# Twenty-seven of the first feed-forward matrix's 32 blocks as seven half-size products for eight

## The chip, the core and the metric

The kernel runs on one core of a Trainium2 chip. TensorE multiplies (weights stationary, tokens moving, sums in PSUM); ScalarE, VectorE and GpSimd do the elementwise work; SyncE (SP) issues most transfers from memory. Each engine works through its own queue. The metric is the time of one execution on the device in microseconds. Three runs of the kernel before took 1827.59, 1828.64 and 1833.59 us; their median is 1828.64 us.

## The reference

One layer of a recurrent decoder trunk for a prompt of 256 tokens and 8 samples of 4 tokens, 288 tokens in all, with a model width of 2048. Everything is float32. The part at issue is the last one, the feed-forward with its norm and its conditioned shift, scale and gate:

```python
mod = jax.nn.silu(c) @ P['w_ada'] + P['b_ada']
sh1, sc1, gt1, sh2, sc2, gt2 = [m[:, None, :] for m in jnp.split(mod, 6, axis=-1)]
...
x = x + gt1 * mix
xn = rmsnorm(x, P['g_norm2']) * (1.0 + sc2) + sh2
x = x + gt2 * (jnp.square(jax.nn.relu(xn @ P['w_ff1'])) @ P['w_ff2'])
...
y = rmsnorm(x, g_final)
```

`w_ff1` is 2048 x 8192 and `w_ff2` 8192 x 2048. Both are read once, for all 288 tokens.

## The kernel before

Features lie on the 128 partitions and the 288 tokens along the free axis (`N` = 288). A float32 product is made of three float16 products: a weight tile of 128 x 1024 is converted to a high part by ScalarE (`to_parts`, L210) and a low part by VectorE (`rest`, L134, one scalar-tensor-tensor operation that also writes a column of sums for a later check), the tokens are split the same way, and TensorE adds high x high, high x low and low x high in PSUM (L301).

The feed-forward (`feed_forward`, from L2001) goes over 256 *visits*. A visit is one weight tile of 128 x 1024, 512 KB, and 24 matmuls of 128 x 128 weights with 288 columns of tokens. The hidden width is cut into eight parts `hb`. For each there are four blocks of the first matrix (`ff1`, 256 outputs each, two PSUM banks, four visits) and four of the second (`ff2`, 512 outputs, four banks, four visits). `order` lists them: the first matrix for part `hb`, then the second for part `hb - 1`. A first-matrix block ends in `ev` of `ff1`: relu and square on ScalarE, a square and the low part on VectorE, into the tiles `hx`. A second-matrix block is added into the accumulator `facc` by VectorE (L1940), for the first part by ScalarE copies (L1936).

At step `v` the program first lets `convert` run until the tiles of five visits are ahead, then multiplies visit `v`, then evacuates a block that is complete. `convert` of one tile issues the transfer of a later tile into the buffer that it frees (`fetch`, on SP's queue). `in_order` chains the instructions of TensorE, ScalarE and VectorE in the order in which the program issues them; GpSimd's are ordered by the planner. PSUM has eight banks: four of the pool `mm`, two `px`, one `pi`, one `pa`.

Beside the visits run the last units of the adaLN product, those of the gate `gt2`: each loads 1 MB of `w_ada`, and `step` acts on letters that are repeated over the visits: L loads a unit, C converts a part of it, v multiplies it. In `cond_parts` a unit is converted to float16 parts (ScalarE L449, VectorE L134) and multiplied in 16 float16 matmuls (L466); in `cond_product` it is multiplied as float32, without conversion (L418). `half_resid` multiplies the accumulator by the gate and adds the residual on GpSimd (L1924 to L1927), at the end of the second matrix's blocks of part 6. `certificates` checks the columns of sums from all low parts against bounds with some VectorE operations and small matmuls (L144 to L150); if a bound is missed, the whole trunk is run a second time in a slower form.

Ahead of the feed-forward, `scaled` (L1857) and `sumsq` (L638) work on GpSimd for the second norm, and `second_norm` (L1895 to L1899) produces the tokens' two parts `zh` and `zl` in the first four steps.

Of the kernel before, what the change touches and what calls it, by code (L numbers as in the profile page):

```python
# [8 lines left out]
F32 = mybir.dt.float32  # L9
# [45 lines left out]
def trunk(ctx, tc, io, fast):  # L55
# [96 lines left out]
    def certificates():  # L152

        yield from certify(0, mixed[0], 8.0)
        yield from certify(704, mixed[1], 2.0 ** -3)
        done_ = list(mixed)
        for at_ in (150, total - 24, total - 5):
            while now[0] < at_:
                yield
            upto = list(marks)  # L160
            yield from certify(done_[0], upto[0], 8.0)
            if upto[1] > done_[1]:
                yield from certify(done_[1], upto[1], 2.0 ** -3)
            done_ = upto
# [101 lines left out]
    def in_order():  # L266
# [4 lines left out]
        for i in traced[n:]:  # L271
# [3 lines left out]
            if i.engine in (mybir.EngineType.PE, mybir.EngineType.Activation, mybir.EngineType.DVE):  # L275
                queued[i.engine] = i
# [8 lines left out]
    class Block:  # L285

        def __init__(self, w, blk, g0, width, act, evac):
            self.w, self.blk, self.g0, self.act, self.evac = w, blk, g0, act, evac
            self.nm_t, self.kg = width // P, 1024 // width
            self.ps = None  # L290

        def multiply(self, g, hi, lo, ms, kks):
            if self.ps is None:
                self.ps = [bank() for _ in range(self.nm_t)]
            hi, lo = (t_.rearrange("p (k m) -> p k m", k=self.kg) for t_ in (hi, lo))
            for m in ms:
                for kk in kks:
                    k = self.kg * g + kk
                    xh, xl = self.act(k)
                    for i, (a, x) in enumerate(((hi, xh), (hi, xl), (lo, xh))):  # L300
                        pace["last"] = T.matmul(self.ps[m][:, :N], a[:, kk, m * P:(m + 1) * P], x, start=k == 0 and i == 0,  # L301
                                                stop=k == 4 * self.kg - 1 and i == 2)

# [210 lines left out]
    def ada_half(name, kind, h):  # L514
# [6 lines left out]
        if fast and name != "sj0":  # L521
# [1388 lines left out]
    def ff1(hb):  # L1910
        for b in range(4):
# [8 lines left out]
            yield Block(io["wf1"], 4 * hb + b, 0, 256, lambda k: (zh[:, k, :], zl[:, k, :]), ev)  # L1920
# [8 lines left out]
    def ff2(hb):  # L1929
        x = hx[hb % 2]  # L1930
        for b in range(4):
            def ev(m, p, b=b):
# [6 lines left out]
                if hb < 7:  # L1939
                    V.tensor_tensor(out=a, in0=a, in1=p, op=ALU.add)  # L1940
                    if hb == 6:
# [6 lines left out]
            yield Block(io["wf2"], b, 4 * hb, 512, lambda k: (x[0][:, k, :], x[1][:, k, :]), ev)  # L1948

    blocks = []  # L1950
    for hb in range(9):
        if hb < 8:
            blocks.extend(ff1(hb))
        if hb:
            blocks.extend(ff2(hb - 1))
# [218 lines left out]
```

## Time and profile before

| | |
|---|---|
| median of three runs | 1828.64 us (1827.59 to 1833.59) |
| profiled execution, its time | 1828.35 us |
| profiled execution, span from first to last instruction | 1826.6 us |
| mean granted TensorE clock | 0.991 |
| instructions | 38533 |

The span is that of one execution; the 1.75 us that its time has beyond it lie around the first and the last instruction. In the rows that follow, PE is TensorE, PEld its weight loads, ACT is ScalarE, DVE is VectorE and POOL is GpSimd. A row of a group has the line of the program, engine and operation, output and inputs with shapes and types, the count, then busy time in us and mean ns of one, then the idle time ahead of it with what ended it. A row of the timeline begins with the start and the duration in us. A row of a stretch has its bounds, its length, and the busy time of PE, PEld, DVE, ACT and POOL with their counts, then the clock, the DMA share and GB/s.

### The profile page before, as it was taken

To read this page: it belongs to the slowest core of one execution; us is meant where nothing else is said; L and a number is where in the kernel's file an instruction comes from. 1 tells how busy PE (TensorE), PEld (TensorE's weight loads), DVE (VectorE), ACT (ScalarE), POOL (GpSimd) and SP (SyncE) were. 2 spreads that over 40 slices of the span, in tenths; PEclk is the share of its full clock that TensorE was granted. 3 is DMA by queue.
4 is the path that set the end of the run, shared out by engine and by line. 5 is a ranking of instruction groups with operands and counts; after the bars stand their busy time and mean duration, and the time that the engine had idled before them with its cause. 6 is when DMAs were issued, how large, how long until landed. Compare 5 with 4: busy or idle time off the path is not lost.

```text
span 1826.6 us, 38533 instructions
## 1 busy us (share of the span) xinstructions
PE 1775.3 (97%) x15792; PEld 1377.2 (75%) x15792; DVE 1183.4 (65%) x2568; ACT 901.8 (49%) x1252; POOL 211.2 (12%) x281
## 2 busy tenths in 40 slices
PE   8999999999999999999999899999999999999996
PEld 6787667786777877677777677777777777777785
DVE  4777855645685568687677876556665566555565
ACT  5334384545455455366555565554544454443443
POOL 0002201110133010001113500000000000000171
PEclk9999999999999999999999899999999999999998
DMA  9999767547855459977778556566656556555541
GB/s 392 414 410 337 262 226 258 208 155 268 282 177 184 163 197 323 312 242 261 252 286 316 184 195 198 197 204 215 204 198 217 203 197 203 173 183 176 184 151 55
DMA packets 113290, 422.97 MB, mean 232 GB/s; under 512 B 11648, under 2 KB 11936, under 8 KB 109904
## 3 DMA queue, kind: packets, MB, share of 16 engines
q1 hardware_dynamic: 97744, 364.18, 56.7%
q0 software_dynamic: 10608, 39.64, 6.2%
q10 hardware_dynamic: 4752, 16.60, 2.3%
q8 instruction: 125, 2.05, 0.4%
q14 instruction: 61, 0.50, 0.1%
HBM read 403.56 MB, written 16.81 MB: 230 GB/s over the span
## 4 chain that ended last, share of the span: by engine, by line
PE 65%; DVE 2%; DMA 1%; issue 1%; ACT 1%; POOL 0%; DVEq 0%; ACTq 0%; POOLq 0%
PE mm L301 33%; PE mm L237 20%; PE pi L301 8%; PE pa L466 1%; DMA st<-mC 1%; DVE pair L134 0%; PE px L1629 0%; DMA s<-mC 0%; PE px L1715 0%; DMA o_C_s<-st 0%; PE pi L1698 0%; PE px L1639 0%; DVE s L2051 0%; PE px L1570 0%; PE px L1558 0%
## 5 line engine op out<-in xcount | busy, mean ns | idle before, releaser
L237 PEld LDWEIGHTS <-pair 128*128 128x128 f16 x6528 | 631.8, 98 | 202.3 <-issue 22.0
L301 PEld LDWEIGHTS <-pair 128*128 128x128 f16 x6144 | 601.3, 98 | 159.4 <-issue 7.1
L237 PE MATMUL mm<-x,pair 128*128 128x288 f16 x4320 | 563.3, 287 | 7.1 <-DVE pair L134 2.8
L134 DVE SCALAR_TENSOR_TENSOR pair<-raw,pair 128x1024 f16<-128x1024 f32 x250 | 308.3, 1235 | 224.4 <-ACT pair L224 130.5
L301 PE MATMUL mm<-hx,pair 128*128 128x288 f16 x2472 | 321.0, 286 | 0.0
L301 PE MATMUL mm<-z,pair 128*128 128x288 f16 x2448 | 313.4, 288 | 3.3 <-ACT z L1899 2.9
L134 DVE SCALAR_TENSOR_TENSOR pair<-xl,pair 128x1024 f16<-128x1024 f32 x165 | 202.9, 1231 | 150.1 <-ACT pair L224 91.1
L224 ACT ACTIVATE pair<-raw 128x1024 f16<-128x1024 f32 x163 | 171.6, 1054 | 217.4 <-PE mm L237 136.5
L134 DVE SCALAR_TENSOR_TENSOR pair<-s,pair 128x1024 f16<-128x1024 f32 x113 | 140.2, 1242 | 123.2 <-ACT pair L210 123.1
L224 ACT ACTIVATE pair<-xl 128x1024 f16<-128x1024 f32 x109 | 114.9, 1054 | 164.2 <-PE mm L237 96.4
L210 ACT ACTIVATE pair<-s 128x1024 f16<-128x1024 f32 x113 | 119.0, 1054 | 142.7 <-PE mm L301 109.3
L210 ACT ACTIVATE pair<-raw 128x1024 f16<-128x1024 f32 x87 | 91.5, 1054 | 124.2 <-PE mm L301 86.1
L237 PE MATMUL mm<-y,pair 128*128 128x288 f16 x768 | 99.4, 289 | 3.4 <-ACT ag L1361 3.4
L210 ACT ACTIVATE pair<-xl 128x1024 f16<-128x1024 f32 x56 | 58.8, 1054 | 80.0 <-PE mm L301 68.4
L237 PE MATMUL mm<-mrg,pair 128*128 128x288 f16 x768 | 95.3, 286 | 0.1
L1924 POOL TENSOR_SCALAR s<-s,mod 128x256 f32<-128x256 f32 x16 | 14.8, 928 | 665.7 <-DVE s L1940 665.7
L301 PE MATMUL pi<-hx,pair 128*128 128x288 f16 x600 | 89.8, 286 | 0.0
L301 PE MATMUL pi<-z,pair 128*128 128x288 f16 x624 | 85.0, 286 | 0.0
L237 PE MATMUL mm<-s,pair 128*128 128x288 f16 x384 | 49.6, 286 | 0.0
L237 PE MATMUL px<-x,pair 128*128 128x288 f16 x288 | 42.1, 287 | 3.9 <-DVE pair L134 3.3
L134 DVE SCALAR_TENSOR_TENSOR xl<-xl,uh 128x1024 f16<-128x1024 f32 x30 | 40.6, 1354 | 0.0
L1393 POOL TENSOR_TENSOR s<-s,t 128x288 f32<-128x288 f32 x16 | 19.7, 1261 | 152.0 <-DVE t L1392 152.0
(478 smaller groups left out, 1586.1 us busy)
## 6 DMA issues: line engine op xcount, KB each, us to landing
raw<-win SPq DMA_DIRECT2D x115, 512.0 KB, 5.4
s<-wf SPq DMA_DIRECT2D x113, 512.0 KB, 3.5
raw<-wf SPq DMA_DIRECT2D x87, 512.0 KB, 3.4
xl<-win SPq DMA_DIRECT2D x77, 512.0 KB, 5.1
xl<-wf SPq DMA_DIRECT2D x56, 512.0 KB, 3.5
s<-wq SPq DMA_DIRECT2D x20, 1024.0 KB, 13.0
xl<-wada SPq DMA_DIRECT2D x16, 1024.0 KB, 6.1
s<-wada SPq DMA_DIRECT2D x13, 1024.0 KB, 6.7
```

The lines of the kernel that those rows point to most:

```text
L134: return V.scalar_tensor_tensor(dst, src, scale, hi if fast else hi.bitcast(F32), op, ALU.subtract, accum_out=mark(w))
L210: pace["hi"] = S.activation(hi, raw, AF.Copy, scale=WS)
L224: pace["hi"] = S.activation(hi, raw, AF.Copy, scale=WS)
L237: pace["last"] = T.matmul(ps, w[:, kk, ms], x, start=k == k0 and i == 0, stop=k == kt - 1 and i == 2)
L301: pace["last"] = T.matmul(self.ps[m][:, :N], a[:, kk, m * P:(m + 1) * P], x, start=k == 0 and i == 0, stop=k == 4 * self.kg - 1 and i == 2)
L466: pace["prod"] = T.matmul(ps[32 * j:32 * j + 32, a:a + 256], silp[:, 32 * k:32 * k + 32], v[:, j], start=q == i == n == 0, stop=q == KT // ...
L1393: (V if br == 1 else G).tensor_tensor(out=a, in0=a, in1=t, op=ALU.add)
L1924: G.tensor_scalar(a[:, 0:NP], a[:, 0:NP], mod[:, GT2, k, 0:1], None, ALU.mult)
```

## The change

Five blocks of the first matrix stay as they are (all four of part 0 and the first of part 1). The other 27 are computed by a scheme of seven products in place of eight: the block's 512 x 256 weight tile of a visit is cut into 2 x 2 quarters, and the tokens into two halves of 144 (`H`). With four sums of weight quarters and four differences of token quarters, seven products of half the size in each direction give the four quarters of the output. A visit of such a block has 7 x 2 x 3 = 42 matmuls with 144 columns.

The weights are laid out by quarters beforehand (`quadrants`); the transfer is 512 KB as before, into the first 1024 columns of a tile of 2304. GpSimd writes the sums into the tile (`weight_sums`, four operations of 256 columns, two steps after the transfer was issued), and the conversion then covers 1792 columns on ScalarE and on VectorE. The tokens' differences are made once, for eight pairs of feature tiles, in the steps 4 to 13 (`differences`: one addition on VectorE and GpSimd by turns, four subtractions on GpSimd; two steps later the split on ScalarE and VectorE). The output of a block lies in three banks, which one ScalarE copy and four VectorE additions bring together (`ev` in `seven`).

Visits of the seven products and of the second matrix alternate in pairs. An evacuation is issued one step later than before (`later`), after that step's conversions. The converted tiles go round a ring of eight, of which a tile of seven products takes two. GpSimd's instructions now are chained in program order too. The units of the gate are multiplied as float32, a load every 15 visits into one buffer, the product four visits later. `half_resid` moves to the last 20 visits, and all checks to the last 15.

```diff
-        yield from certify(0, mixed[0], 8.0)
-        yield from certify(704, mixed[1], 2.0 ** -3)
-        done_ = list(mixed)
-        for at_ in (150, total - 24, total - 5):
-            while now[0] < at_:
-                yield
-            upto = list(marks)
-            yield from certify(done_[0], upto[0], 8.0)
-            if upto[1] > done_[1]:
-                yield from certify(done_[1], upto[1], 2.0 ** -3)
-            done_ = upto
+        upto = list(marks)
+        yield from certify(704, upto[1], 2.0 ** -3)
+        yield from certify(0, upto[0], 8.0)
...
-            if i.engine in (mybir.EngineType.PE, mybir.EngineType.Activation, mybir.EngineType.DVE):
+            if i.engine in (mybir.EngineType.PE, mybir.EngineType.Activation, mybir.EngineType.DVE) or fast and i.engine == mybir.EngineType.Pool:
...
+        def col(self, kk, m):
+            return 256 * ((1, 0), (2, 3))[kk % 2][m] + P * (kk // 2) if self.quad else (self.nm_t * kk + m) * P
...
+    S3, A11, A12, A22, S1, S2, S4 = range(0, 1792, 256)
+
+    class Seven:
+
+        def __init__(self, blk, forms, evac):
+            self.w, self.blk, self.g0, self.forms, self.evac = io["wf1"], blk, 0, forms, evac
+            self.ps = None
+
+        def multiply(self, g, hi, lo):
+            if self.ps is None:
+                self.ps = misc(), misc(), longp()
+            for a, b, i in ((A11, 0, 0), (S2, 0, 2), (A12, 0, 1), (S3, 1, 1), (S1, 1, 0), (A22, 2, 1), (S4, 2, 0)):
+                p = self.ps[b][:, H * i:H * i + H]
+                for j in range(2):
+                    xh, xl = self.forms(a, 2 * g + j)
+                    c = a + P * j
+                    for n, (w, x) in enumerate(((hi, xh), (hi, xl), (lo, xh))):
+                        pace["last"] = T.matmul(p, w[:, c:c + P], x, start=g == j == n == 0 and a in (A11, S3, A22),
+                                                stop=g == 3 and j == 1 and n == 2, skip_group_check=True)
...
-        if fast and name != "sj0":
+        if fast and kind != GT2 and name != "sj0":
...
+    def differences(k, E):
+
+        z = sp.tile([P, 1028], F32, tag="st", name=nm("st"), bufs=2)
+        e = [z[:, H * i:H * i + H] for i in range(5)]
+        E.tensor_tensor(out=z[:, 0:2 * N].rearrange("p (a n) -> p a n", a=2), in0=zh[:, 2 * k:2 * k + 2, :], in1=zl[:, 2 * k:2 * k + 2, :], op=ALU.add)
+        for o, a, b in ((4, 3, 1), (1, 1, 0), (3, 3, 1), (2, 2, 3)):
+            G.tensor_tensor(out=e[o], in0=e[a], in1=e[b], op=ALU.subtract)
+        yield
+        h, l = (zt[0][:, i, k, :] for i in range(2))
+        S.activation(h, z[:, H:5 * H], AF.Copy)
+        rest(l, z[:, H:5 * H], 1.0, h)
+
+    def forms(a, k):
+        if a in (A11, A12, S4):
+            n, c = {A11: (0, 0), A12: (1, 0), S4: (1, H)}[a]
+            return tuple(t[:, 2 * k + n, c:c + H] for t in (zh, zl))
+        n = {S1: 0, A22: 1, S2: 2, S3: 3}[a]
+        return tuple(zt[0][:, i, k, H * n:H * n + H] for i in range(2))
+
+    def seven(hb, b):
+        def ev(pa_, pb, pc):
+            e = sp.tile([P, 1028], F32, tag="st", name=nm("st"), bufs=2)
+            q = e[:, 0:5 * H].rearrange("p (a n) -> p a n", a=5)
+            c = e[:, 0:4 * H]
+            two = lambda p, i: p[:, H * i:H * i + 2 * H].rearrange("p (a n) -> p a n", a=2)
+            o = e[:, 5 * H:6 * H]
+            S.activation(o, pa_[:, 0:H], AF.Copy)
+            V.tensor_tensor(out=q[:, 0:5:4], in0=o.unsqueeze(1).to_broadcast([P, 2, H]), in1=two(pa_, 1), op=ALU.add)
+            V.tensor_tensor(out=q[:, 1:4:2], in0=q[:, 4:5].to_broadcast([P, 2, H]), in1=two(pb, 0), op=ALU.add)
+            V.tensor_tensor(out=q[:, 1:3], in0=q[:, 1:4:2], in1=two(pc, 0), op=ALU.add)
+            V.tensor_tensor(out=q[:, 3], in0=q[:, 3], in1=pb[:, 0:H], op=ALU.add)
+            hi, lo = (flat(t[:, 2 * b:2 * b + 2, :]) for t in hx[hb % 2])
+            S.activation(c, c, AF.Relu, scale=1.0 / (WS * ZS))
+            S.activation(hi, c, AF.Square)
+            S.activation(c, c, AF.Square)
+            rest(lo, c, 1.0, hi)
+        return Seven(4 * hb + b, forms, ev)
...
+                    if hb == 6 and not fast:
                         half_resid(x, a, k)
...
+    if fast:
+        own = lambda: pm.tile([P, 512], F32, tag="mm", name=nm("mm"))
+        blocks = [next(ff1(0, (b,), misc if b == 2 else own)) for b in range(4)] + list(ff1(1, (0,), misc)) + [next(ff2(0))]
...
+    plain = len(order)
+    if fast:
+        for hb in range(1, 8):
+            second = list(ff2(hb - 1))
+            for b in range(int(hb == 1), 4):
+                w = seven(hb, b)
+                for g in (0, 2):
+                    order += [(w, g), (w, g + 1), (second[b], g), (second[b], g + 1)]
+        order += [(b, g) for b in ff2(7) for g in range(4)]
...
+    wide = [flat(slot(i)) for i in (2, 3, 8, 9)] if fast else []
...
+        Q.dma_start(t[:, 0:1024], b.w[b.blk, b.g0 + g])
         raws[i] = t
+        if isinstance(b, Seven):
+            due.append((step_[0] + 2, i))
+
+    due, step_ = [], [0]
+
+    def weight_sums(v):
+
+        step_[0] = v
+        while due and due[0][0] <= v:
+            t = raws[due.pop(0)[1]]
+            q = lambda c: t[:, c:c + 256]
+            for o, x, op, y in ((S1, S3, ALU.add, A22), (S3, A11, ALU.subtract, S3), (S2, S1, ALU.subtract, A11), (S4, A12, ALU.subtract, S2)):
+                G.tensor_tensor(out=q(o), in0=q(x), in1=q(y), op=op)
...
+        for k, i in enumerate(deep):
+            then_.setdefault(deep[k - 4] if k > 3 else max(10, last_of.get(k, 0)), []).append(i)
...
+        ring_ = [wp.tile([P, 2048], F16, tag="pair", name=nm("pair"), bufs=5) for _ in range(5)]
+        ring_ += [sp.tile([P, 2048], F16, tag="uh", name=nm("uh"), bufs=3) for _ in range(3)]
...
+            if isinstance(order[i][0], Seven):
+                assert i not in [j for _, j in due]
+                pairs[i] = [next_parts()[:, 0:1792] for _ in range(2)]
+                to_parts(raws.pop(i)[:, 0:1792], *pairs[i])
...
+        if isinstance(b, Seven):
+            b.multiply(g, *t)
+            if g == 3:
+                later.append(lambda: b.evac(*b.ps))
+                if ss[0] > total - 22:
+                    finish_later()
+            return
...
+                if plain <= ss[0] < total - 17 and fast:
+                    later.append(lambda b=b, m=m: b.evac(m, b.ps[m][:, :N]))
+                else:
+                    b.evac(m, b.ps[m][:, :N])
...
+                weight_sums(v)
...
+                finish_later()
                 multiply(ss)
-                now[0] = s
-                if fast and v >= 12:
+                if fast and 4 <= v < 14:
+                    if not zt:
+                        zt.append(extra["xl"].bitcast(F16).rearrange("p (i k c) -> p i k c", i=2, k=8))
+                    if v > 5:
+                        next(half_made.pop(0), None)
+                    if v < 12:
+                        half_made.append(differences(v - 4, V if v % 2 else G))
+                        next(half_made[-1])
+                if fast and s >= total - 15:
                     next(proof, None)
-            yield
-
-    result, mixed, proof = [], list(marks), certificates()
+                    if s % 2:
+                        next(proof, None)
+                if fast and s >= total - 20 and s % 4 == (total - 20) % 4 and s < total - 4:
+                    b = (s - total + 20) // 4
+                    for k in range(4 * b, 4 * b + 4):
+                        half_resid(x2[k // 8][:, k % 8, :], facc[k // 8][:, k % 8, :], k)
...
-        slots.update(ids=("x", None), n=0)
-        every("L . . . . . C . C . . v", skip=8)
+        slots.update(ids=(None,), n=0)
+        every("L . . . v" + 10 * " .", skip=8)
...
+    def quadrants(w):
+        n, g = w.shape[0:2]
+        w = w.reshape(n, g, P, 2, 2, 2, P).transpose(0, 1, 2, 4, 5, 3, 6)
+        return np.ascontiguousarray(np.stack([w[:, :, :, k, m] for k, m in ((0, 1), (0, 0), (1, 0), (1, 1))], 3)).reshape(n, g, P, 1024)
```

`places` and `convert` are otherwise as `then_` and `started` say: which tile's conversion frees the buffer of which later tile. `kernel` passes `quadrants(pack(...))` for `wf1`.

More of the change, by code (lines that the diff above doesn't have):

```diff
@@ L1908, in trunk, with ff1 @@
     tail = {}
-    def ff1(hb):
-        for b in range(4):
+    def ff1(hb, bs=range(4), banks=bank):
+        for b in bs:
             def ev(m, p, b=b):
@@ L1947, in ev @@
                     S.activation(x, x, AF.Copy, scale=Pm("gf")[:, k:k + 1])
[L1948 to L1955, printed above, removed]
-    order = [(b, g) for g in range(4) for b in blocks[0:2]] + [(b, g) for b in blocks[2:] for g in range(4)]
+            yield Block(io["wf2"], b, 4 * hb, 512, lambda k: (x[0][:, k, :], x[1][:, k, :]), ev, *((lambda: pm.tile([P, 512], F32, tag="mm", name=nm("mm")),) if fast else ()))
@@ L1960, in trunk, with is_deep @@
+    wide = [flat(slot(i)) for i in (2, 3, 8, 9)] if fast else []
     homes = [flat(slot(3))[:, 0:2048]]
     if fast:
-        homes = [flat(slot(8))[:, 0:2048], extra["xl"][:, 0:2048]] + homes
+        homes = [wide[i][:, 0:2048] for i in (2, 0, 1)]
     homes = [t[:, a:a + 1024] for t in homes for a in range(0, t.shape[1], 1024)] + [None] * 3
-    raws, pairs, places = {}, {}, []
+    def is_deep(i):
+        return fast and i >= 16 and order[i][0].w is io["wf1"]
+    home, n = [], 0
+    for i in range(total):
+        if is_deep(i):
+            h = n % 4
+            n += 1
+        elif not fast:
+            h = 3 + (i - 3) % len(homes) if i > 2 else None
+        else:
+            h = 3 + (i - 3) % len(homes) if 2 < i < 12 else None
+        home.append(h)
@@ new lines, in places @@
+    def places():
+        narrow = [i for i in range(total) if not is_deep(i)]
+        deep = [i for i in range(total) if is_deep(i)]
+        if not fast:
+            first_ = list(range(len(homes)))
+            return first_, {i: [i + len(homes)] for i in range(total)}
+        then_, started = {}, []
+        users = {}
+        for i in narrow:
+            key = ("r", None)
+            if home[i] is not None and homes[home[i] - 3] is not None:
+                key = ("h", (home[i] - 3) // 2, (home[i] - 3) % 2)
+            users.setdefault(key, []).append(i)
+        r = users.pop(("r", None))
+        for k, i in enumerate(r):
+            if k < 3:
+                started.append(i)
+            else:
+                then_.setdefault(r[k - 3], []).append(i)
+        last_of = {}
+        for key, l in users.items():
+            for k, i in enumerate(l):
+                if k == 0:
+                    started.append(i)
+                else:
+                    then_.setdefault(l[k - 1], []).append(i)
+            w_ = (2, 0, 1)[key[1]]
+            last_of[w_] = max(last_of.get(w_, 0), l[-1])
+        for k, i in enumerate(deep):
+            then_.setdefault(deep[k - 4] if k > 3 else max(10, last_of.get(k, 0)), []).append(i)
+        return sorted(started), then_
```

64 lines of the change are left out of this document (45 added, 19 removed).

## Prediction

> **What bounds the kernel now.** I read the page first, then the busy times by stretch, then the groups of ScalarE and VectorE in the feed-forward with what ended their idle time, then single rows of the timeline.
>
> ```profile
> span 1826.6 us, 38533 instructions
> PE 1775.3 (97%) x15792; PEld 1377.2 (75%) x15792; DVE 1183.4 (65%) x2568; ACT 901.8 (49%) x1252; POOL 211.2 (12%) x281
> ```
> ```profile
> 1100.00:1710.00 610.00, 610.00 (x5119) 483.74 (x5119) 367.28 (x733) 289.33 (x355) 0.00 (x0) 1.00 0.59 197
> 1710.00:1785.00 75.00, 75.00 (x616) 60.02 (x614) 46.10 (x93) 32.04 (x38) 40.62 (x51) 1.00 0.47 155
> ```
> ```profile
> 1100.25 1.63 PE L301 MATMUL mm<-z,pair 128*128 128x288 f16 x12
> 1101.72 1.63 PE L301 MATMUL pi<-z,pair 128*128 128x288 f16 x12
> ```
> ```profile
> L210 ACT ACTIVATE pair<-raw 128x1024 f16<-128x1024 f32 x68 | 71.7, 1055 | 100.5 <-PE mm L301 73.0 <-PE pi L301 25.6 <-DMA s<-wf 1.9
> L134 DVE SCALAR_TENSOR_TENSOR pair<-raw,pair 128x1024 f16<-128x1024 f32 x67 | 82.1, 1225 | 75.1 <-ACT pair L210 75.1
> ```
>
> In the stretch from 1100 to 1710 us TensorE has no idle time at full clock, VectorE is busy 60%, ScalarE 47% and GpSimd 0%. Twelve matmuls start every 1.47 us: 122.5 ns each, so a visit of 24 takes 2.94 us. ScalarE idles for TensorE and VectorE for ScalarE: the feed-forward is bound by matmuls, and GpSimd is free.
>
> **Part 1: fewer columns.** Of the first matrix's 32 blocks 27 change, 108 visits. Each loses 24 matmuls of 288 columns and gets 42 of 144. Removed: 108 x 24 x 122.5 ns = 317.5 us. Added: 4536 matmuls at a pitch that no row of float16 shows. In proportion it would be 61 ns; the weight load sets the upper end:
>
> ```profile
> L301 PEld LDWEIGHTS <-pair x6144: 95/98/181, 1040.1 to 1809.6; 128*128 128x128 f16 x199
> ```
> ```profile
> L1238 PEld LDWEIGHTS pi<-s,st x48: 186/192/192, 369.5 to 399.4; 128*128 128x128 f32 x48
> ```
> ```profile
> 369.76 0.41 PEld L1238 LDWEIGHTS pi<-s,st 128*128 128x128 f32 x3
> ```
> ```profile
> 369.76 0.33 PE L1238 MATMUL pi<-s,st 128*128 128x64 f32 x2
> ```
>
> A load takes 98 ns, and one goes with every matmul. If loads exclude each other, the pitch is 98 ns. But three float32 loads of 192 ns fit in 0.41 us, so they start (0.41 - 0.19)/2 = 0.11 us apart: some 80 ns of each overlap the next, and two matmuls of 275 ns there start 55 ns apart. A float16 load less 80 ns leaves about 18 ns, far under 61. I take 62.5 ns (nearest this row; ends 61 and 98): 283.5 us, **-34.0 us**. A visit of seven products takes 42 x 62.5 = 2.63 us. The change breaks even on matmuls at 317.5/4536 = 70 ns.
>
> The Trainium skill, "TensorE: Matmul & The Clock Gate", section "Back-to-back issue gap", speaks against this: load-matmul pairs sustain about 81 ns at 128 columns. By it, as an estimate, this part would be 367 - 317 = +50 us. Its two figures (131 ns at 512) would put 288 columns at 102 ns; the rows show 122.5. No run here shows 144; the rule is the third rival below.
>
> **Part 2: the gate's units.** The last adaLN product leaves the split path: its units are now 16 float32 records where they were 16 float16 ones.
>
> ```profile
> 534.75 1.63 PE L237 MATMUL mm<-x,pair 128*128 128x288 f16 x12
> 536.31 1.07 PE L418 MATMUL pa<-xl,silc 128*32 128x256 f32 x16
> 537.32 1.40 PE L237 MATMUL mm<-x,pair 128*128 128x288 f16 x10
> ```
> ```profile
> 1116.76 1.63 PE L301 MATMUL mm<-z,pair 128*128 128x288 f16 x12
> ...
> 1118.87 1.40 PE L301 MATMUL mm<-z,pair 128*128 128x288 f16 x10
> ```
>
> ```profile
> L449 ACT ACTIVATE uh<-xl 128x1024 f16<-128x1024 f32 x14 | 14.6, 1041 | 0.0
> L449 ACT ACTIVATE uh<-ag 128x1024 f16<-128x1024 f32 x12 | 12.5, 1040 | 0.0
> ```
>
> After 12 x 0.1225 us the next weight matmul is 1.10 us late with float32 and 0.64 us with float16. Thirteen units lie in the feed-forward (26 conversions, two to a unit): 13 x 0.46 = **+6.0 us**. Their conversions vanish from ScalarE and VectorE, which have other work instead. Their loads now share one buffer, but each load is issued eleven visits after the product that frees it, so SP's queue, and the weights behind it, does not stop: 0.
>
> **Part 3: what takes the matmuls' place.** Visits now come as S S P P S S P P (S seven products, P second matrix), 2 x 11.13 = 22.26 us for eight where it was 23.5. All three other engines run in program order, GpSimd too. I follow the chain from the end of visit 6, when the block's three banks close, to visit 3 of the next eight, which reuses the second matrix's four banks. TensorE needs 2 x 2.94 + 2 x 2.63 = 11.13 us between.
>
> ```profile
> L1917 ACT ACTIVATE hx<-t 128x288 f16<-128x288 f32 x54 | 23.9, 443 | 1.7
> ```
> ```profile
> L134 DVE SCALAR_TENSOR_TENSOR hx<-t,hx 128x288 f16<-128x288 f32 x54 | 24.7, 458 | 6.0 <-DVE t L1918 0.5
> L1940 DVE TENSOR_TENSOR s<-s,mm 128x288 f32<-128x288 f32 x64 | 25.7, 448 | 0.0
> ```
> ```profile
> 1502.80 1.04 ACT L210 ACTIVATE pair<-s 128x1024 f16<-128x1024 f32 x1
> 1503.74 1.04 ACT L449 ACTIVATE uh<-ag 128x1024 f16<-128x1024 f32 x1
> ```
> ```profile
> 1500.15 1.23 DVE L134 SCALAR_TENSOR_TENSOR pair<-raw,pair 128x1024 f16<-128x1024 f32 x1 [0.21 <-ACT pair L210]
> 1501.30 0.08 DVE L134 DVE_READ_ACCUMULATOR pair<-raw,pair 128x1 f32 x1
> ```
>
> ScalarE takes 0.83 ns per column more (443 to 1055), VectorE 1.04 (458 to 1225): 1792 columns are 1.69 and 2.03 us; back to back 0.1 us overlaps. In order: 0.2 start, 1.06 high part of a P tile, 1.18 its low part, three sums of 288 from PSUM one after another 1.44, the fourth of 144 0.33, relu of 576 0.70, two squares 1.18, high part of the next P tile 0.95, of an S tile 1.69, its low part 1.98, the first sum into the accumulator 0.50. That is **11.2 us against 11.13**: the cover is gone even before GpSimd interferes. It does:
>
> ```profile
> 1732.56 1.54 POOL L1927 TENSOR_TENSOR s<-s,s 128x288 f32<-128x288 f32 x2
> ```
> ```profile
> 1734.07 2.52 POOL L1927 TENSOR_TENSOR s<-s,s 128x288 f32<-128x288 f32 x2
> ```
> ```profile
> 1734.21 1.73 DVE L134 SCALAR_TENSOR_TENSOR pair<-raw,pair 128x1024 f16<-128x1024 f32 x1 [1.71 <-ACT pair L210]
> ```
> ```profile
> 527.41 0.74 POOL L863 TENSOR_TENSOR s<-s 128x256 f32<-128x256 f32 x1
> ```
> ```profile
> s<-wf SPq DMA_DIRECT2D x113, 512.0 KB, 3.5
> ```
>
> Two GpSimd operations take 1.54 us alone and 2.52 beside a low part, and the low part takes 1.73 instead of 1.23: while one reads, the other stands, 0.50 us per collision, 0.45 for 256 columns. Sums from PSUM (L1940) are not touched. An S visit brings four GpSimd operations of 0.74 us, 3.0 us. Their tiles are fetched when the low part of an earlier S tile frees the buffer (1.4 us before the chain begins, and 1.3 after) and land 3.5 us later, 2 and 5 us into the chain, behind what earlier sets left over. The sums themselves are needed only some six visits later, so their lateness costs nothing; but GpSimd asks between nearly all low parts. The P part is 0.45 late outright; the low part of 576, the next P part and the S part are 0.45 late each, of which ScalarE's own time hides some 0.8. I take 1.0 us in all (ends 0 and 1.8, four full collisions): TensorE stands 1.1 us in each eight visits. Of 27 such blocks the first three evacuate by ScalarE copies and escape: 24 x 1.1 = **+26.4 us**. Twelve gate units come among these blocks, one in 15 visits, so each a place earlier in its block than the one before; eight fall between visit 6 and visit 3, where TensorE would stand: 8 x 1.1 = **-8.8 us**.
>
> The Trainium skill, "SBUF — State Buffer", section "Who interferes with whom", has the loser blocked for the whole instruction. By that a collision would cost up to 0.74 us and the stalls, as an estimate, some 15 us more; the row shows 0.50 where the GpSimd operation takes 0.77, and the measurement decides.
>
> **Part 4: the edges.** The first sixteen weight sums stand on GpSimd's queue ahead of the tokens' differences, 16 x 0.74 = 12 us, and ScalarE waits for the second difference; its conversions are four visits, 11.8 us, ahead: +2 us (0 to 6). Before the feed-forward, conversions of gate units stood in VectorE's way and GpSimd's:
>
> ```profile
> 1017.66 1.36 DVE L134 SCALAR_TENSOR_TENSOR xl<-xl,uh 128x1024 f16<-128x1024 f32 x1
> ...
> 1021.60 1.53 DVE L134 SCALAR_TENSOR_TENSOR xl<-xl,uh 128x1024 f16<-128x1024 f32 x1
> ```
> ```profile
> 1016.70 10.75 POOL L1857 TENSOR_SCALAR s<-s,mod 128x256 f32<-128x256 f32 x4 [0.96 <-DVE mod L495]
> ```
> ```profile
> 1036.79 0.75 PE L645 MATMUL pi<-row,ones 128*128 128x288 f32 x2 [2.95 <-POOL row L638]
> ```
>
> These four go; the first-matrix tiles are converted some 5 us earlier, and GpSimd reaches the sum that TensorE waits 2.95 us for: -3 us (-8 to 0). The checks' sums, all moved to the last fifteen visits, are the same work beside matmuls: 0. GpSimd's share of the last residual (most of the 40.6 us between 1710 and 1785) moves to the last 20 visits, 58.8 us, and each quarter is issued seven visits ahead of the sum that needs it: 0; without that cover the last blocks' sums would wait.
>
> Sum: -34.0 + 6.0 + 26.4 - 8.8 + 2 - 3 = **-11.4 us**. The profiled execution took 1828.35 us (span 1826.6), 0.3 under the median of 1828.64: 1828.35 - 11.4 = **1817 us**.
>
> **Rivals.** *Clean overlap*: the low parts slip between GpSimd's reads (against it: GpSimd has work in nearly every gap). Then 27 x 0.1 stays of the stalls: -34.0 + 6.0 + 2.7 + 1 - 3 - 1 = -28: **1800 us**. *VectorE becomes the bound*, slower: its eight visits hold 4 x 1.95 (S low parts) + 4 x 1.15 (P) + 1.77 (sums of seven) + 0.68 (their low part) + 4 x 0.37 (sums into the accumulator) = 16.3 us, and in order it must wait some 2.0 us for relu and squares: 18.3. Each GpSimd operation that stops it adds 0.45, of 16. Against the 23.5 us of now, and 0.3 for gate units that it would hide, it decides from 12 of 16 on. At 14 it is 24.6 us: 24 x 24.6 + 3 x 22.3 - 27 x 23.5 = +23; less 7.7 for twelve units of 0.64 us then hidden, and 1 at the edges: **1842 us** (at all 16, 1864). For it: GpSimd is hardly ever idle. Against it: several of its operations fall into VectorE's waits and its sums from PSUM. *Loads bound the matmuls*, from 70 ns on: at 98 ns Part 1 is +127 us; the longer S visits cover all stalls; with Part 2 and the edges **1960 us**; half-way between the ends, at 80 ns, 1878 us. For it: 98 ns in 75% of the span; against it: the overlapping float32 loads. *The check fails*: the kernel falls into its second, slow pass, over 3600 us; nothing in the profile speaks for it.
>
> **Chances.** Forecast 0.56 (1806 to 1834), clean overlap 0.25, VectorE bound 0.11, loads 0.07, slow pass 0.01. Under 0.3%, 5.5 us, this kernel's runs can't be told apart. Faster by more (below 1822.9): the clean case and 0.34 of the forecast, 0.59; within: the forecast's other 0.22; slower: the last three, 0.19. The range 1797 to 1838 takes in both ends of the collisions and leaves out the last three.
>
> **What would show it.** Right: matmuls of 144 columns 62 to 63 ns apart; TensorE idle about 1 us before the second matrix's blocks, released by VectorE's L1940 sums; low parts of 1792 columns at 2.0 us, often 2.5; GpSimd 50% busy or more. Wrong: no idle time of TensorE there (clean), or idle ahead of every visit for low parts (VectorE), or a pitch over 70 ns.

## The result and the profile after

| | before | after |
|---|---|---|
| median, us | 1829.53 (1827.59 to 1833.59, 4 runs) | 1852.16 (1848.22 to 1857.15, 4 runs) |
| ratio, 95% interval | 1 | 1.0122 [1.0101, 1.0143] |
| span of the profiled run, us | 1826.6 | 1850.3 |

The change made the kernel 1.2% slower; 1817 us had been predicted. Two of the runs below hold one timing each far outside their others (2745 us in c4_all_on_gpsimd, 6416 us in c5_one_block_later), which the ratios leave out and the medians do not; what they were isn't known.

In the profile after, line numbers differ: L296 is the matmul of a plain block, L317 that of the seven products, L202 a high part, L134 a low part, L1996 the sum into the accumulator, L2073 GpSimd's sums of weights, L1944 and L1946 the tokens' differences, L1949 their split. First the head of the page:

```profile
span 1850.3 us, 42916 instructions
PE 1759.9 (95%) x17728; PEld 1410.8 (76%) x17728; DVE 1328.8 (72%) x2502; ACT 946.6 (51%) x1228; POOL 795.0 (43%) x749
```

TensorE is busy 15 us less in a span that is 24 us longer, so some 39 us of idle time are new; GpSimd went from 211 to 795 us busy, VectorE from 1183 to 1329. Where the time went is seen by counting matmuls: the k-th of the feed-forward's 256 visits begins after the same number of matmuls in every run, so its start can be compared with the same visit of before.

| us | before | after | difference |
|---|---|---|---|
| first matmul of the feed-forward | 1042.0 | 1044.2 | +2.3 |
| from there to the first seven products (24 visits) | 76.9 | 93.3 | +16.4 |
| the stage of 27 x 8 visits | 643.8 | 646.2 | +2.4 |
| the last 16 visits | 47.1 | 49.8 | +2.7 |

The differences are of unrounded times, and their sum is +23.8. The last row goes to the start of the last matmul. The stage that was to win 10 us won nothing, and the 24 visits ahead of it lost most of the rest. What TensorE waited for, by the view of waits, in the stage (1140 to 1758 us) and at the start (1030 to 1140); the columns are total, number and longest:

```profile
PE mm L296 <- DVE s L1996: 23.4, 18, 1.9
PE mm L296 <- ACT s L1992: 0.9, 2, 0.7
```
```profile
PE mm L296 <- ACT z L1915: 3.9, 3, 1.8
PE mm L296 <- DVE pair L134: 2.6, 1, 2.6
PE mm L296 <- ACT uh L202: 2.3, 1, 2.3
PE pa L434 <- DMA ag<-wada: 1.9, 1, 1.9
PE pi L661 <- POOL row L654: 1.2, 1, 1.2
PE mm L296 <- DVE uh L134: 1.1, 1, 1.1
```

In the stage nearly all waiting is for the sums into the accumulator (L1996); the rest is for the copies that the first part has in their place (L1992). At the start there are many, for conversions on ScalarE and VectorE. The busy times by stretch show what came on top; the clock is the number after POOL's. Before:

```profile
1060.00:1100.00 40.00, 38.71 (x313) 30.50 (x311) 29.10 (x75) 23.21 (x39) 0.97 (x4) 1.00 0.60 210
1100.00:1120.00 20.00, 20.00 (x176) 15.72 (x176) 15.57 (x39) 12.23 (x17) 0.00 (x0) 1.00 0.56 176
```

After:

```profile
1060.00:1100.00 40.00, 37.44 (x288) 28.63 (x287) 30.14 (x78) 21.11 (x40) 15.33 (x23) 0.96 0.42 146
1100.00:1140.00 40.00, 31.91 (x239) 22.47 (x238) 29.30 (x45) 20.10 (x28) 34.12 (x37) 0.87 0.44 136
```

From 1100 to 1140 TensorE is busy 31.9 of 40 us at a mean clock of 0.87, GpSimd 34.1 us where it had nothing to do before. By stretches of 5 us the clock is 0.66 in three of the eight, from 1105, 1120 and 1130 us, and 1.00 in the others: as an estimate, up to 3 x 5 x 0.34 = 5 us of the 16.4 are the slower clock. The waits for conversions and for the gate's load above (2.6, 2.3, 1.9 and 1.1 us) are 7.9 more. What ScalarE waited for (1040 to 1140 us) names the queue:

```profile
ACT xl L1949 <- POOL st L1946: 22.6, 6, 7.2
```
```profile
1112.00 1.04 ACT L202 ACTIVATE pair<-raw 128x1024 f16<-128x1024 f32 x1
1120.29 0.68 ACT L1949 ACTIVATE xl<-st 128x576 f16<-128x576 f32 x1 [7.25 <-POOL st L1946]
1120.88 1.04 ACT L202 ACTIVATE uh<-raw 128x1024 f16<-128x1024 f32 x1
```

These rows of ScalarE's timeline read: the split of a difference stands 7.25 us for GpSimd, and a conversion of weights that needs nothing from it stands behind it in program order.

### The profile page after: what moved, and what is told of

It reads as the page before. It is cut to its first block, busy times and chain, and to the rows that moved or that the text cites. A ratio compares the mean times of both kernels' runs of the same rounds, so it can differ in the third digit from the quotient of the medians.

```text
span 1850.3 us, 42916 instructions
## 1 busy us (share of the span) xinstructions
PE 1759.9 (95%) x17728; PEld 1410.8 (76%) x17728; DVE 1328.8 (72%) x2502; ACT 946.6 (51%) x1228; POOL 795.0 (43%) x749
## 3 DMA queue, kind: packets, MB, share of 16 engines
q8 instruction: 141, 2.31, 0.5%
## 5 line engine op out<-in xcount | busy, mean ns | idle before, releaser
L229 PEld LDWEIGHTS <-pair 128*128 128x128 f16 x6528 | 631.5, 98 | 202.2 <-issue 22.0
L2073 POOL TENSOR_TENSOR s<-s 128x256 f32<-128x256 f32 x432 | 553.7, 1299 | 84.4 <-DMA s<-wf 62.4
L134 DVE SCALAR_TENSOR_TENSOR pair<-raw,pair 128x1024 f16<-128x1024 f32 x249 | 333.9, 1347 | 145.4 <-ACT pair L216 132.9
L296 PEld LDWEIGHTS <-pair 128*128 128x128 f16 x2232 | 218.9, 99 | 96.5 <-issue 36.9
L296 PE MATMUL mm<-hx,pair 128*128 128x288 f16 x1896 | 242.0, 287 | 30.4 <-DVE s L1996 26.0
L317 PEld LDWEIGHTS <-pair 128*128 128x128 f16 x3038 | 204.9, 98 | 4.6 <-issue 1.7
L134 DVE SCALAR_TENSOR_TENSOR pair<-xl,pair 128x1024 f16<-128x1024 f32 x109 | 134.3, 1233 | 91.3 <-ACT pair L216 91.0
L202 ACT ACTIVATE pair<-s 128x1792 f16<-128x1792 f32 (+1 forms) x88 | 143.3, 1640 | 109.2 <-issue 55.3
L296 PEld LDWEIGHTS <-uh 128*128 128x128 f16 x1320 | 129.8, 99 | 41.3 <-issue 3.1
L296 PE MATMUL mm<-hx,uh 128*128 128x288 f16 x1176 | 151.5, 288 | 3.4 <-ACT uh L202 2.3
L134 DVE SCALAR_TENSOR_TENSOR pair<-s,pair 128x1792 f16<-128x1792 f32 (+1 forms) x62 | 136.1, 2198 | 23.3 <-ACT pair L202 20.4
L317 PE MATMUL px<-xl,pair 128*128 128x144 f16 x1302 | 114.4, 226 | 0.0
L317 PEld LDWEIGHTS <-uh 128*128 128x128 f16 x1498 | 107.4, 98 | 1.1 <-issue 0.4
L202 ACT ACTIVATE pair<-raw 128x1024 f16<-128x1024 f32 x86 | 88.5, 1049 | 36.5 <-PE pi L317 17.1
L134 DVE SCALAR_TENSOR_TENSOR uh<-s,uh 128x1792 f16<-128x1792 f32 (+1 forms) x30 | 66.5, 2220 | 28.2 <-ACT uh L202 28.1
L317 PE MATMUL px<-z,pair 128*128 128x144 f16 x868 | 84.2, 226 | 0.2 <-DVE pair L134 0.2
```

Source lines behind the costliest of these rows:

```text
L134: return V.scalar_tensor_tensor(dst, src, scale, hi if fast else hi.bitcast(F32), op, ALU.subtract, accum_out=mark(w))
L202: pace["hi"] = S.activation(hi, raw, AF.Copy, scale=WS)
L229: pace["last"] = T.matmul(ps, w[:, kk, ms], x, start=k == k0 and i == 0, stop=k == kt - 1 and i == 2)
L296: pace["last"] = T.matmul(self.ps[m][:, :N], a[:, c:c + P], x, start=k == 0 and i == 0, stop=k == 4 * self.kg - 1 and i == 2)
L317: pace["last"] = T.matmul(p, w[:, c:c + P], x, start=g == j == n == 0 and a in (A11, S3, A22), stop=g == 3 and j == 1 and n == 2, skip_gro ...
L2073: G.tensor_tensor(out=q(o), in0=q(x), in1=q(y), op=op)
```

## The experiments

All are edits of the changed kernel. "Start" is the time from the feed-forward's first matmul to the 24th visit's end less the 76.9 us of before; "stage" is the time of the 216 visits behind it. The runs e1 to e6 were executed once each, c2 to c5 five or six times. Executions of one kernel spread by 6 to 11 us here, so the readings rest on the start and the stage within one trace, and a small difference of the span says nothing.

| run | start, us | stage, us | span, us |
|---|---|---|---|
| before | 0 | 643.8 | 1826.6 |
| after | 16.4 | 646.2 | 1850.3 |
| e1_sums_first | 15.4 | 627.1 | 1835.5 |
| e2_no_weight_sums | 8.4 | 620.5 | 1818.6 |
| e3_split_later | 3.3 | 654.0 | 1848.6 |
| e4_gate_later | 16.1 | 644.9 | 1849.6 |
| e5_start_and_end | 11.9 | 643.3 | 1843.7 |
| e6_no_differences | 2.3 | 643.6 | 1836.8 |
| c2_all_orders | 12.1 | 619.8 | 1822.7 |
| c3_two_on_vector | 11.5 | 622.2 | 1821.3 |
| c4_all_on_gpsimd | 1.7 | 630.5 | 1821.4 |
| c5_one_block_later | 1.4 | 620.9 | 1809.3 |

**The stage: order or collisions?** The first run changes the order alone.

```diff
                 weight_sums(v)
+                finish_later()
                 while made < ss[0] + depth:
                     convert(made)
                     made += 1
-                finish_later()
```

> Edit: in each visit the evacuations that stand waiting are issued ahead of the next conversions, not behind them; nothing else changes. Theory (the queue's order makes the stall): in the stage of seven products the 27 gaps of TensorE in front of the second matrix's blocks (1.4 to 2.1 us each, 31 us in all) fall under 0.3 us each, since the four sums of 0.45 us then start at most one low part (2.5 us) after the last product of the old block, and TensorE needs 5.3 us for the two visits between: the span goes from 1850 to about 1820 us. Rival (VectorE is simply too busy in these visits): the idle time stays within 10 us of what it was and only moves, to waits of matmuls for the low parts of weights. The start of the feed-forward (first seven-product visit at 1137.5 us against 1118.9 in the kernel before the change) stays within 2 us.

The waits of TensorE from 1140 to 1755 us are now

```profile
PE pa L434 <- DMA ag<-wada: 6.8, 8, 1.7
PE mm L296 <- DVE s L1996: 0.5, 2, 0.3
```

The gaps went from 23.4 us of waits to 0.5, and the stage is 19 us shorter, not 30: a new wait, that of the gate's products for their own loads, took 6.8, and the gap behind the stage's last visit grew from 1.6 to 3.9 us. The span is 1835.5, not 1820, for these and because this run reached the feed-forward 3.9 us later than the run of after. VectorE was not the bound. The second run takes GpSimd's reads away:

```diff
-            t = raws[due.pop(0)[1]]
-            q = lambda c: t[:, c:c + 256]
-            for o, x, op, y in ((S1, S3, ALU.add, A22), (S3, A11, ALU.subtract, S3), (S2, S1, ALU.subtract, A11), (S4, A12, ALU.subtract, S2)):
-                G.tensor_tensor(out=q(o), in0=q(x), in1=q(y), op=op)
+            i = due.pop(0)[1]
+            if i < 30:
+                G.memset(raws[i][:, 1024:1792], 0.0)
```

> Leaves out GpSimd's sums of weights (432 operations of the stage; the three summed quarters of each tile are zeros, so the output is not the reference's). Theory (GpSimd's reads stretch VectorE's low parts from 2.0 to 2.5 us and that makes the stall): the gaps in front of the second matrix's blocks fall from 1.4 to 2.1 us to 0.1 to 0.4, some 25 to 31 us in all. At the start the 16 sums between 1111 and 1136 us go as well: the first seven-product visit comes 3 to 8 us earlier than 1137.5. Span about 1817 us. Rival (the order of VectorE's queue alone makes the stall, whatever GpSimd does): gaps of 1.0 us or more stay, 24 us or more in all, and the span stays above 1835.

The gaps fell to 0.2 us each (0 to 0.7), about as expected, and the first seven-product visit came 6.1 us earlier. The groups by shape, 1150 to 1755 us, show what GpSimd's reads do; the last number before the second bar is the mean in ns. After:

```profile
L134 DVE SCALAR_TENSOR_TENSOR pair<-s,pair 128x1792 f16<-128x1792 f32 x51 | 117.8, 2312 | 23.3 <-ACT pair L202 20.4 <-issue 2.6
L2073 POOL TENSOR_TENSOR s<-s 128x256 f32<-128x256 f32 x411 | 528.1, 1303 | 77.7 <-DMA s<-wf 56.6 <-DVE pair L134 4.3 <-DVE hx L134 0.7
```

Without the sums of weights:

```profile
L134 DVE SCALAR_TENSOR_TENSOR pair<-s,pair 128x1792 f16<-128x1792 f32 x52 | 105.9, 2036 | 46.5 <-ACT pair L202 33.2 <-issue 13.2
```

With the order of e1_sums_first, where the gaps are gone:

```profile
L134 DVE SCALAR_TENSOR_TENSOR pair<-s,pair 128x1792 f16<-128x1792 f32 x53 | 131.6, 2496 | 1.3 <-ACT pair L202 1.3
```

So a gap needs both: the low part of a wide tile ahead of the sums in VectorE's order, and GpSimd's reads that stretch the chain. In e1_sums_first the low parts are longest of all (2.50 us), and nothing waits for them, because they are five visits early and the sums are not behind them.

**The start.** Two runs change who waits for whom.

```diff
-        z = sp.tile([P, 1028], F32, tag="st", name=nm("st"), bufs=2)
+        z = flat(facc[k % 6 // 3])[:, 720 * (k % 3):720 * (k % 3) + 720]
...
-                if fast and 4 <= v < 14:
+                if fast and 4 <= v < 17:
...
-                    if v > 5:
+                    if v > 8:
```

> Edit: the tokens' differences keep their work, but their sums lie in six buffers of the accumulator's memory (idle there) in place of two, and ScalarE's split of each is issued five visits after its sums in place of two. Theory (ScalarE's queue stands behind GpSimd's differences, and the conversions of weights behind it): ScalarE's six waits for GpSimd (22.6 us) shrink under 4 us, TensorE's waits for conversions at 1098.9, 1115.9, 1123 and 1128 us and the slower clock after them go, and the first seven-product visit comes 8 to 13 us earlier than 1137.5; the span about 1840. Rival (the three narrow buffers and their loads set the pace): ScalarE then waits for loads of weights instead, and the visit comes less than 4 us earlier. Rival (GpSimd and VectorE stop one another): both are as late as before, less than 4 us as well.

The first seven-product visit came 10 us earlier, as the queue's theory said. But ScalarE still waited 13.9 us for GpSimd up to 1140 us, not under 4, and the first eight visits of the stage took 10.6 us longer than their matmuls (1.1 of it a gate unit), so that the span was 1848.6 and not 1840. Two rows of TensorE's waits (1060 to 1165 us) and two of GpSimd's timeline:

```profile
PE px L317 <- DVE pair L134: 2.6, 2, 2.1
PE px L317 <- ACT pair L202: 2.3, 1, 2.3
```
```profile
1128.82 2.18 POOL L1946 TENSOR_TENSOR s<-s 128x144 f32<-128x144 f32 x4
1130.96 34.43 POOL L2073 TENSOR_TENSOR s<-s 128x256 f32<-128x256 f32 x27
```

GpSimd ends its last difference at 1131 us, 3.5 us after the seven products began, and has 34 us of sums of weights in front of it. ScalarE's queue had passed on GpSimd's lateness; without it the lateness comes out later, at another place.

```diff
-        every("L . . . v" + 10 * " .", skip=8)
+        every("L . . . v" + 10 * " .", skip=24)
```

> Edit: the gate's units in the feed-forward begin 16 matmul groups later, so that none falls between the first visits and the first seven products. Theory (the first unit's product stood waiting 1.9 us for its own load and brought a slower clock, 1.7 us more): the first seven-product visit comes 3 to 5 us earlier than 1137.5, and as the unit's own 1.1 us is only moved, the span falls 2 to 4 us. Rival (the time is lost anyway, because the conversions behind it are late): the wait turns up at the next conversion, and the visit comes at most 1.2 us earlier, the span within 1.5 us of 1850.

The rival held: 0.3 us at the start, 0.7 in the span. The gate's unit filled time that was lost anyway.

```diff
+                        G.memset(extra["xl"][:, 0:4608], 0.0)
-                    if v > 5:
-                        next(half_made.pop(0), None)
-                    if v < 12:
-                        half_made.append(differences(v - 4, V if v % 2 else G))
-                        next(half_made[-1])
```

> Leaves out the tokens' differences altogether (their place holds zeros, written once by GpSimd), so the output is not the reference's. Theory (the differences and the queues behind them made the late start): of 16.4 us of lateness between the start of the feed-forward and the first seven-product visit at most 5 stay, 1.9 to 4 of them the gate's unit; the three clock halvings at 1106, 1120 and 1130 us go except the unit's own. Rival (the loads into three narrow buffers, or the conversions, are late by themselves): 10 us or more stay. The stage behind keeps its 31 us of gaps.

2.3 us of the start's 16.4 stay, and the stage keeps its gaps (643.6 us). So the differences, with what stood behind them, cost 14 us. e2_no_weight_sums shows 8 us for the sums of weights in the same place: the two prices overlap, since either alone would have found room. Could VectorE take some of it?

```diff
-            G.tensor_tensor(out=e[o], in0=e[a], in1=e[b], op=ALU.subtract)
+            E.tensor_tensor(out=e[o], in0=e[a], in1=e[b], op=ALU.subtract)
...
-                        half_made.append(differences(v - 4, V if v % 2 else G))
+                        half_made.append(differences(v - 4, V if v >= 8 else G))
...
-        return fast and i >= 16 and order[i][0].w is io["wf1"]
+        return fast and i >= 16 and (order[i][0].w is io["wf1"] or i >= total - 16 and i % 2 == 1)
```

> Edit of the changed kernel at two places that lie far apart in time. Start: the tokens' differences in six buffers and split five visits later, as in e3_split_later, and besides the last four of the eight differences are made by VectorE alone, so that GpSimd makes four and then the sums of weights. End: every second tile of the last 16 loads goes to one of the four wide buffers, which stand empty there, in place of the three narrow ones. Theory (GpSimd had more to do at the start, 35 us of differences and 19 us of sums of weights, than it could do in time; whoever came later waited): the lateness of the first seven-product visit against the start of the feed-forward, 16.4 us in the changed kernel, falls under 5 us, and the first eight visits of the stage no longer stand 9 us as they did in e3_split_later. Rival (the work itself is too much for these 20 visits, whoever does it): VectorE's low parts of weights are late instead, and 10 us or more remain at the end of the first eight visits. End: the gap of 1.6 us in front of the last block's first visit goes, if the three narrow buffers made it (ScalarE waited 5 us for a load there); it stays, if GpSimd's share of the residual makes it. Span 1833 to 1841 us, the stage's 31 us of gaps staying.

The start stayed 11.9 us late, so the theory's number was wrong and the rival's right. TensorE waited 3.0 us for a low part on VectorE and 3.0 us for a gate unit's load; e4_gate_later had shown that taking the unit away alone gains nothing. The end gained too little to tell (its gap of 1.6 us became 1.1, in one execution).

All orders together, with the gate's units later (`"L . . . . . . . v" + 6 * " ."`, 24 skipped):

> Edit: the order of e1_sums_first, both edits of e5_start_and_end, and the gate's units later: the first 16 matmul groups later, and each unit's product seven groups behind its load in place of four. Theory (the gaps of the stage, the late start and the late end are three separate losses, and the seven products themselves save 34 us): the losses of 31, some 12 and 4 us are nearly all gone, the span is 1800 to 1812 us, and the ratio to the kernel before 0.985 to 0.991. Rival (VectorE, then busy some 20 of 22.3 us in eight visits, becomes the bound once the others are gone): waits for low parts of weights appear in front of the stage's visits, and the span stays above 1820.

Median 1821.96 us against 1832.98, ratio 0.9944 [0.9920, 0.9968]: faster than both kernels, but the span is 1822.7, above the 1800 to 1812 expected and on the rival's side of 1820. The rival's waits for low parts did not come in the stage, though. The stage is 24 us shorter than before; the start still lost 12, of which TensorE waited

```profile
PE mm L296 <- DVE pair L134: 5.7, 1, 5.7
PE px L296 <- DVE pair L134: 2.6, 1, 2.6
```

Two runs move the differences between the engines, `v >= 10` in the line above and `G` for all.

> Edit of c2_all_orders: of the eight differences GpSimd makes six and VectorE the last two (four and four there). In c2_all_orders TensorE stood 8.3 us at the start for low parts that were late on VectorE, while GpSimd stood 25.6 us. Theory (at the start GpSimd and VectorE together are short of time, and what is late follows where the differences are put): VectorE is 2 x 2 to 2 x 4 us less burdened, GpSimd ends six differences at about 1106 us and its first sums of weights still ahead of their use at 1132; the wait of 8.3 us falls under 3, the first seven-product visit comes 5 to 8 us earlier than 1137.0, the median 1814 to 1818 us. Rival (the low parts are late because loads into the three narrow buffers reach ScalarE late, 6.8 us at 1085 to 1092): the wait stays above 6 us and the time within 2 us of c2_all_orders.

Its rival named the outcome, not the cause: 1821.83 us, 0.9948 [0.9926, 0.9969], and VectorE had no idle time from 1093 to 1125 us, so no load held it up. What grew were its operations. Four differences and an addition on VectorE while GpSimd rested, in c2_all_orders:

```profile
1099.84 0.75 DVE L1944 TENSOR_TENSOR s<-z 128x576 f32<-128x576 f16 x1
1100.62 1.33 DVE L1946 TENSOR_TENSOR s<-s 128x144 f32<-128x144 f32 x4
```

and in c3_two_on_vector, while GpSimd worked without a pause, from 1104 us on at 16 sums of weights in a row:

```profile
1098.33 2.28 DVE L134 SCALAR_TENSOR_TENSOR pair<-s,pair 128x1024 f16<-128x1024 f32 x1
1103.91 1.03 DVE L1944 TENSOR_TENSOR s<-z 128x576 f32<-128x576 f16 x1
1104.97 3.08 DVE L1946 TENSOR_TENSOR s<-s 128x144 f32<-128x144 f32 x4
```
```profile
1104.28 16.19 POOL L2073 TENSOR_TENSOR s<-s 128x256 f32<-128x256 f32 x16
```

Four differences of VectorE take 3.08 us in place of 1.33, and a low part of 1024 columns 2.28 in place of 1.22. Summed over VectorE's rows from 1096.9 to 1118.7 us, the excess over the undisturbed durations is 9.1 us, and TensorE stood 8.2 us for two low parts, one among these rows and one behind them. Work moved from GpSimd to VectorE in these visits is paid on both.

> Edit of c2_all_orders: GpSimd makes all eight differences, VectorE none. Theory (as for c3_two_on_vector: what is late follows where they are put): TensorE no longer waits for VectorE's low parts at the start, but GpSimd, with 8 x 4.5 us of differences from 1075 on and sums of weights between, ends them at 1120 to 1130 and the sums of the first blocks later still: the first seven products wait 3 to 9 us for conversions of summed weights, as in e3_split_later (9 us), and the median is 1816 to 1822 us. Rival (only VectorE is short): no such wait, and the median is under 1815.

As expected: the start lost only 1.7 us, the stage lost 10.8 us more than in c2_all_orders, nearly all of it in its first sixteen visits, and the median is 1821.79 us (0.9946 [0.9924, 0.9967]). Three ways to divide the same work gave the same time: start and first sixteen visits of the stage together lose 12.1, 11.5 and 12.2 us. The last run gives it room instead:

```diff
-        blocks = [next(ff1(0, (b,), misc if b == 2 else own)) for b in range(4)] + list(ff1(1, (0,), misc)) + [next(ff2(0))]
+        blocks = [next(ff1(0, (b,), misc if b == 2 else own)) for b in range(4)] + [x for p in zip(ff1(1, (0, 1), misc), ff2(0)) for x in p]
...
-            for b in range(int(hb == 1), 4):
+            for b in range(2 * (hb == 1), 4):
```

> Edit of c4_all_on_gpsimd: one block more of the first matrix (six in place of five) stays a plain block, so that the seven products begin eight visits later; all differences by GpSimd. That gives back 34/27 = 1.3 us of columns. Theory (at the start the differences and the sums of weights share GpSimd and stop VectorE at the same time; eight visits more put them one behind the other): the 8 us that TensorE stands in the stage's first eight visits in c4_all_on_gpsimd fall under 1.5, the lateness of the first seven-product visit against the start of the feed-forward stays under 4 us, and the median is 1814 to 1817 us, ratio 0.990 to 0.993. Rival (the wait comes from something else at the stage's first visits, such as the loads into the wide buffers): it moves with the stage's begin and the median is 1822 us or more.

As expected: 1814.04 us, ratio 0.9891 [0.9874, 0.9907]. The start is 1.4 us late and the stage's first eight visits wait for nothing; TensorE's waits from 1060 to 1170 us are what the normalisation always cost:

```profile
PE mm L296 <- ACT z L1915: 1.6, 1, 1.6
PE mm L296 <- DVE z L134: 0.6, 2, 0.3
```

## Why the prediction was wrong

**The step that failed** most is Part 4, the start: "+2 us (0 to 6)". It measured +16.4. It priced one queue, twelve microseconds of weight sums on GpSimd ahead of the differences, against conversions four visits ahead, and it gave the differences themselves no price. The order was wrong too: GpSimd's first sum of weights started at 1111.34 us, behind six of the eight differences. The differences have three prices. GpSimd's groups from 1060 to 1140 us after show the first:

```profile
L1946 POOL TENSOR_TENSOR st<-st 128x144 f32<-128x144 f32 x32 | 24.2, 759 | 11.8 <-DVE st L1944 9.6
L2073 POOL TENSOR_TENSOR s<-s 128x256 f32<-128x256 f32 x16 | 16.7, 1055 | 0.6
L1944 POOL TENSOR_TENSOR st<-z 128x576 f32<-128x576 f16 x4 | 6.5, 1632 | 4.7 <-DVE xl L134 4.7
```

That is 30.7 us of differences beside 16.7 of weight sums. The second is VectorE's share, with both engines stretching one another; the third the splits in ScalarE's order in front of the conversions, with which the cover of four visits ran out (22.6 us of waits). e6_no_differences (14 us less) shows the differences as the cause; e2_no_weight_sums (8 us less), c3, c4 and c5 show that the lack was of time on GpSimd and VectorE together.

**Part 3's stall was mis-sized**: "TensorE stands 1.1 us in each eight visits", 26.4 us less 8.8. The mechanism, the place and the releaser (VectorE's sums into the accumulator, here L1996) were right. So was the credit of the gate's units: the nine blocks with such a unit in the chain, or behind ScalarE's copies, have gaps of 0 to 0.8 us, 2.8 together. But the other seventeen measured 1.36 to 2.06 us, mean 1.58, so that the gaps are 17 x 1.58 + 2.8 = 29.7 us where 17.6 were forecast, 16 blocks of 1.1. The term that was too small is the 1.0 us for collisions, taken from the ends 0 and 1.8: without them the gap is 0.2 (e2_no_weight_sums), so they weighed 1.4.

Which of its parts was off, the number of collisions or the 0.8 us that ScalarE was to hide, isn't taken apart. The price of one was read from a single meeting, a low part of 1.73 us and two GpSimd operations of 2.52. One by one, the first of these two had begun 0.14 us ahead of the low part and took its usual 0.79, and the low part lost 0.50. The second began inside the low part, ended 0.65 us behind it and took 1.77. So the two lost 0.50 and 0.98 us there, not 0.50 each, and when they meet decides how much.

**The end** was put at 0 twice, for the checks and for GpSimd's share of the residual. The last 16 visits took 2.7 us more; four places at the checks' matmuls make some 2 of it, one with a wait:

```profile
1803.17 0.43 PE L146 MATMUL px<-gd,ones 128*128 128x55 f32 x2 [0.48 <-DVE gd L144]
```

In front of them a gap of 1.4 us for the sums stands behind conversions whose loads came late (ScalarE waited 16.5 us for loads into three narrow buffers, 1765 to 1833 us, and none before the change). The loads make a part of it at most: in c2_all_orders and c5_one_block_later, where ScalarE has no such wait, the gap is still 1.5 us. Whether GpSimd's share of the residual adds to it wasn't tried apart.

**Before the feed-forward** "-3 (-8 to 0)" was not seen: the wait for the row sum fell as forecast, from 2.95 to 1.24 us, but the feed-forward began 2.3 us later. In the ten other runs with the same edit it began 2.1 to 6.2 us later, partly from loads of state that landed later; with one trace of before this stays open.

**Right** were Part 1 and Part 2. A group of six matmuls of 144 columns begins every 0.375 us, 62.5 ns each:

```profile
1138.21 0.54 PE L317 MATMUL px<-xl,pair 128*128 128x144 f16 x6
1138.58 0.54 PE L317 MATMUL px<-z,pair 128*128 128x144 f16 x6
1138.96 0.91 PE L317 MATMUL px<-xl,pair 128*128 128x144 f16 x12
```

so the 34.0 us are there, and the rival of loads as the bound falls. The Trainium skill, "TensorE: Matmul & The Clock Gate", section "Back-to-back issue gap", gives 81 ns at 128 columns for pairs of load and matmul. This trace shows 62.5 at 144 columns, so the measurement decides against that rule here. A gate unit in float32 costs 1.1 to 1.2 us in the stage, as forecast, and up to 2.8 where its load is late (e1_sums_first).

Together the misses make 34.5 of the 35 us between forecast and result: 14.4 at the start, 12.1 in the gaps, 5.3 ahead of the feed-forward and 2.7 at the end.

Of the rivals, the clean overlap needed GpSimd's reads to cost nothing; e2_no_weight_sums shows what that would have given. VectorE as the bound has the right sign but the wrong place: in the stage VectorE never bounded, even when it was busy 529.6 of 605 us in c2_all_orders, and at the start, where the rival gave the edges -1, it did.

## What to carry to other kernels

Preparing operands for fewer matmuls is work with a place of its own: price the hand-over, the visits in which the new form's operands are made while the old form still runs, engine by engine and queue by queue, before the steady stage. Where two engines stop one another, moving work between them changes which one is late and not by how much; give it more visits, at the price of a block in the old form. And when an evacuation frees what TensorE needs next, issue it ahead of conversions that have visits to spare.

## What the runs showed of the hardware that was not expected

The loss in a collision of GpSimd and VectorE falls on both: low parts of 1792 columns took 2.04 us alone and 2.31 to 2.50 beside GpSimd, a sum of 256 columns on GpSimd 1.30 on average where it takes 0.74 alone, and VectorE's differences of 144 columns 0.77 in place of 0.33, more than twice. Of the 411 sums in the stage of after (1150 to 1755 us) the median took 0.73 us and the longest 2.61. Single operations look like turns: a sum that began at 1346.94 us, inside a low part of 1346.28 to 1348.74, took 2.39 us and ended 0.59 us behind it. At the start of c3_two_on_vector four short operations in a row beside sums of weights lost more in proportion (1.33 to 3.08 us) than a long low part does in the stage (2.04 to 2.50).

Behind idle gaps of 1.9 to 2.6 us at the start TensorE's granted clock fell (mean 0.87 from 1100 to 1140 us), but the gaps of up to 2.1 us in the stage left it at 1.00 (1150 to 1755 us). What makes the difference no run here shows.
